# Gates behind the last SSD projection, transposes ahead of a q projection, and neighbouring blocks in one transfer: one layer of a streaming encoder trunk

## The chip, the cores and the metric

The kernel runs on one core of one Trainium2 chip. Its time is the device time of one launch, in microseconds (us), and a kernel's figure is the median of several launches. Engines are named as the profile names them: PE multiplies matrices, DVE is the vector engine, ACT the scalar engine (functions, copies with a scale), POOL and SP here only issue transfers (DMA). PEclk, or granted clock, is the share of full speed at which PE was allowed to run.

## The reference

One layer takes 576 tokens of width 1024 (512 of a prompt and 64 of a sample, with separate states and memories), and computes three branches from one normed input:

```python
h = _rmsnorm(x, norm_pre_w)
proj = h @ w_in
glu_v, glu_g, conv_gate, z, xbc, dt_raw, q, xa_gate, gates = jnp.split(proj, points, axis=-1)

u = glu_v * jax.nn.sigmoid(glu_g)
c, new_a = _causal_dwconv(u, st_a, conv_dw_w, conv_dw_b)      # width 31
c = jax.nn.silu(_layernorm(c, conv_ln_w, conv_ln_b)) * jax.nn.silu(conv_gate)
out_a = c @ conv_out_w
...
yg = yg * lax.rsqrt(jnp.mean(yg * yg, axis=-1, keepdims=True) + EPS)
y = yg.reshape(bsz, t, D_INNER) * ssd_norm_w.astype(f32)
out_b = y.astype(x.dtype) @ ssd_out_w
...
p = jax.nn.softmax(s, axis=-1)                                # 4 heads of 256, 256 memory tokens
o = jnp.einsum('bhtm,bmhd->bthd', p, mem_v.astype(f32)).reshape(bsz, t, XA_DIM).astype(x.dtype)
out_c = (o * jax.nn.silu(xa_gate)) @ xa_out_w

g = jax.nn.sigmoid(gates + gate_b).reshape(bsz, t, N_BRANCH, D_MODEL)
m = g[:, :, 0] * out_a + g[:, :, 1] * out_b + g[:, :, 2] * out_c
x_new = x + _rmsnorm(m @ w_out, norm_post_w)
```

Everything is float32. The states of both convolutions and of the scan, and keys and values of the memory, are outputs too.

## The kernel before

**Arithmetic.** Every float32 operand of a large product is split into a high part, rounded to the type fp32r, and a low part, the rest; a product is the sum of three matmuls (high by high, high by low, low by high). A projection takes 128 output channels for all tokens: 8 blocks of the inner dimension, 3 matmuls each, in two halves of 288 tokens, 48 matmuls (L214, `proj`) into one PSUM tile `mm`, of which there are two. So a projection waits until the tile of the one before the last has been read out. The right sides `hT` are the transposed normed input, high and low.

**Weights.** `wjob` puts a block of weights on the list `order`; `prep_to` works that list off, two blocks ahead of PE: SP fetches 512 KB into `raw` (three buffers), ACT rounds it into `whi` (L189), and the low part `wlo` comes either from a subtraction on DVE (L191) or from a negated copy on ACT (L193) with a DMA behind it that POOL issues and that adds `raw` to it (L194).

**Stages.** RMSNorm and transposes come first, then the four groups of the SSD branch with other projections between them, to about 510 us. The branch ends with four output projections `out_b(3, q)`. Two jobs stand behind these (L857 to L866): a projection each for `cg0` and `cg1`, the first blocks of the conv gate, of which a silu is made and stored in DRAM. Their silu is a tanh on ACT (L862) and a multiplication on DVE (L863) that reads the PSUM tile too:

```python
nc.scalar.activation(v2(t), va(pt), AF.Tanh, scale=0.5)
nc.vector.scalar_tensor_tensor(v2(t), v2(t), 1.0, va(pt), ALU.add, ALU.mult)
```

**Pairs** (516 to 726 us). Seventeen pairs of 128-column blocks of `w_in` are multiplied by a 2 by 2 block scheme with seven products, P1 to P7, of 12 matmuls each (L937, `product`), in place of eight. The products are summed in the PSUM tiles X, Y and Z, two of each. `slot` runs one product and the reading of its tile (on ACT or DVE, into tiles `ct`, `zs`, `ys`); `seq` lists the 119 slots, in which P2 of the next pair comes ahead of P7 of the present one. Ahead of the products, `pair_load` (L897) fetches the blocks into `raw` and `rawb` (four transfers of 256 KB a pair). `pair_pure` splits a block that enters a product as it is: P1, P2 and P4 have their high part `ph` from ACT (L907), and their low part `pl` from a negated copy on ACT (L908) and an adding DMA of POOL. `pair_sum` makes the sums of blocks that P5, P6, P7 and P3 need: four sums on DVE (L916), two splits on ACT (L919) and DVE (L920).

**Background.** The depthwise convolution is eight channel blocks with 31 taps and a first step each, one DVE instruction a tap (L791). `push_conv` puts its steps on a list, and `bgrun(n)` gives out n of them at the place where it stands; in the pairs that is `if i % 3: bgrun(1)`, in two of three slots.

**Attention** (740 to 880 us). For each head h: `att_kq` (two key projections, each followed by a q projection), `att_pt` for the head before (transposes of its softmax P on PE, L1212 and L1219, and the copies out of PSUM `pth` L1215, `ptl` L1216, `pts` L1221), `att_k` (transposes of keys, L1125 and L1177), `att_out` for the head before (products with the values, L1151 to L1153, L1235), and `att_scores`. A fifth turn ends the fourth head; there `fill` runs projections `cg2` to `cg4` in place of keys.

**Merge, LayerNorm, tail.** Eight merges (L1297, L1298) bring the attention branch into the accumulator `ob`, each with `bgrun(5)`. Eleven late projections follow, the rest of the conv gate `cg` and of the gate `g0` of the conv branch; a `cg` becomes a silu (tanh L474, multiplication L475/L476), a `g0` a tanh. Among them LayerNorm over the channels of the convolution: `ln_mean` sums all channels, and their squares, by matmuls with ones (L1309, L1310), `ln_rstd` takes the root on ACT (L1327) and the reciprocal on DVE (L1328). Then for each of eight channel blocks: multiply (L1359), tanh (L1362), three more DVE steps, and the split in high (L616) and low (L620) parts, on which the conv output projections `oa` work. `out_rows` ends the kernel.

**What sets the order.** The code is written in one sequence, and a scheduler with a simulated timeline then sets the order of the instructions on each engine; `bgrun` steps have a priority of their own. So instructions may stand on an engine some places before or behind where the code has them, and the order of each engine is shown where it matters.

Of the kernel before, what the change touches and what calls it, by code (L numbers as in the profile page):

```python
# [28 lines left out]
def hybrid_trunk_kernel(  # L29
# [829 lines left out]
    for j in range(2):
        pt = proj(f"cg{j}")  # L860
        t = sx.tile([128, 640], F32, tag="bc", name="bc", bufs=4)[:, 0:T]
        nc.scalar.activation(v2(t), va(pt), AF.Tanh, scale=0.5)  # L862
        nc.vector.scalar_tensor_tensor(v2(t), v2(t), 1.0, va(pt), ALU.add, ALU.mult)  # L863
# [24 lines left out]
    def pair_load(p):  # L888
        kind, i = pairs[p]
        cs = (C_GG + 128 * i, C_GV + 128 * i) if kind == "glu" else (base[kind] + 256 * i, base[kind] + 256 * i + 128)  # L890
        for kh in range(2):
# [4 lines left out]
            for n in range(2):  # L896
                nc.sync.dma_start(  # L897
                    out=raw[:, 512 * n:512 * n + 512].rearrange("p (k c) -> p k c", k=4),
                    in_=w_in[512 * kh:512 * kh + 512, cs[n]:cs[n] + 128].rearrange("(k p) c -> p k c", p=128),
                )  # L900
                pw[p][f"W{n + 1}{kh + 1}"] = raw[:, 512 * n:512 * n + 512]

    def pair_pure(p, w, pr):
        src = pw[p][w]
# [3 lines left out]
        nc.scalar.activation(lo, src, AF.Copy, scale=-1.0)  # L908
# [131 lines left out]
    for i, (p, pr) in enumerate(seq):  # L1040
# [469 lines left out]
```

## Time and profile before

| | us |
|---|---|
| three runs | 1125.15, 1127.86, 1120.45 |
| median | 1125.15 |
| the profiled execution | 1124.0 |
| its span in the trace | 1122.3 |
| mean granted clock of its core | 0.994 |
| ACT busy | 614.7 |
| POOL busy | 152.9 |

The profile is of a fourth execution. Its span goes from the first to the last recorded work of the core. A row of a group reads: line, engine, operation, output tile `<-` input tiles, count, then busy time. In brackets behind a row of the chain of waits stands how long the engine was idle ahead of it and what ended that. A row that lists the waits of PE has the total in us, how often, and the longest. Windows list for each engine its busy time and, as x, the instructions that began there, then the granted clock, the share of time in which the DMA engines were busy, and GB/s.

### The profile page before, as it was taken

To read this page: it belongs to the slowest core of one execution; us is meant where nothing else is said; L and a number is where in the kernel's file an instruction comes from. 1 tells how busy PE (TensorE), PEld (TensorE's weight loads), DVE (VectorE), ACT (ScalarE), POOL (GpSimd) and SP (SyncE) were. 2 spreads that over 40 slices of the span, in tenths; PEclk is the share of its full clock that TensorE was granted. 3 is DMA by queue.
4 is the path that set the end of the run, shared out by engine and by line. 5 is a ranking of instruction groups with operands and counts; after the bars stand their busy time and mean duration, and the time that the engine had idled before them with its cause. 6 is when DMAs were issued, how large, how long until landed. Compare 5 with 4: busy or idle time off the path is not lost. (4 is left out here: it accounts for less than half of the span.)

```text
span 1122.3 us, 20511 instructions
## 1 busy us (share of the span) xinstructions
PE 1091.3 (97%) x8081; PEld 1047.8 (93%) x8081; DVE 852.6 (76%) x1353; ACT 614.7 (55%) x1086; POOL 152.9 (14%) x247
## 2 busy tenths in 40 slices
PE   8999999999999999998999999999999999999997
PEld 8999999999999999998999999999999999999974
DVE  5778898578878984698898897669888789575533
ACT  5664675456436543745666656645655633675431
POOL 0100120012002100312323422100000111111000
PEclk9999999999999999998999999999999999999999
DMA  7354433442353235679797698666558698677812
GB/s 208 95 165 118 144 111 103 128 118 80 95 146 96 87 82 131 148 168 211 160 246 175 146 229 211 160 193 171 151 153 198 152 279 199 152 169 177 253 39 84
DMA packets 204086, 172.03 MB, mean 153 GB/s; under 512 B 15222, under 2 KB 176030, under 8 KB 203990
## 3 DMA queue, kind: packets, MB, share of 16 engines
q1 hardware_dynamic: 188006, 128.18, 39.5%
q0 software_dynamic: 14544, 39.59, 19.6%
q10 hardware_dynamic: 1440, 2.95, 0.7%
q8 instruction: 63, 1.03, 0.4%
q14 instruction: 33, 0.27, 0.1%
HBM read 116.49 MB, written 14.62 MB: 117 GB/s over the span
## 5 line engine op out<-in xcount | busy, mean ns | idle before, releaser
L214 PE MATMUL mm<-hT,whi 128*128 128x288 f32 (+2 forms) x2240 | 398.7, 298 | 2.9 <-DVE hi L476 1.3
L214 PEld LDWEIGHTS mm<-hT,whi 128*128 128x128 f32 x2240 | 334.5, 189 | 6.1 <-issue 1.5
L214 PE MATMUL mm<-hT,wlo 128*128 128x288 f32 (+2 forms) x1120 | 247.2, 298 | 0.2 <-DMA wlo<-raw 0.2
L189 ACT ACTIVATE whi<-raw 128x1024 fp32r<-128x1024 f32 x118 | 124.7, 1056 | 200.4 <-PE mm L214 157.6
L791 DVE SCALAR_TENSOR_TENSOR c<-u,dww,c 128x606 f32<-128x606 f32 x240 | 200.4, 844 | 2.5
L214 PEld LDWEIGHTS mm<-hT,wlo 128*128 128x128 f32 x1120 | 185.0, 189 | 1.3 <-issue 0.5
L191 DVE TENSOR_TENSOR wlo<-raw,whi 128x1024 fp32r<-128x1024 f32 x68 | 83.0, 1220 | 43.4 <-ACT whi L189 43.0
L214 PE MATMUL mm<-hi,whi 128*128 128x288 f32 x512 | 111.4, 299 | 0.3 <-DVE lo L1297 0.3
L214 PE MATMUL mm<-lo,whi 128*128 128x288 f32 x512 | 110.6, 296 | 0.0
L214 PE MATMUL mm<-hi,wlo 128*128 128x288 f32 x512 | 110.2, 296 | 0.0
L194 POOL DMA_DIRECT2D wlo<-raw x50 | 43.7, 873 | 396.5 <-ACT wlo L193 311.4
L214 PEld LDWEIGHTS mm<-hi,whi 128*128 128x128 f32 x512 | 82.4, 188 | 1.7 <-issue 1.1
L214 PEld LDWEIGHTS mm<-lo,whi 128*128 128x128 f32 x512 | 82.8, 188 | 0.0
L214 PEld LDWEIGHTS mm<-hi,wlo 128*128 128x128 f32 x512 | 82.7, 188 | 0.0
L193 ACT ACTIVATE wlo<-raw 128x1024 fp32r<-128x1024 f32 x50 | 52.4, 1048 | 16.1 <-PE ps L214 15.1
L466 DVE SCALAR_TENSOR_TENSOR acc<-xp,scw,acc 128x579 f32<-128x579 f32 x72 | 58.3, 813 | 3.1 <-ACT acc L462 1.9
L907 ACT ACTIVATE ph<-rawb 128x512 fp32r<-128x512 f32 x34 | 21.5, 632 | 56.5 <-PE X L937 29.9
L920 DVE TENSOR_TENSOR wlo<-sm,whi 128x1024 fp32r<-128x1024 f32 x34 | 41.4, 1219 | 7.3 <-ACT whi L919 7.3
L458 POOL COPY tails<-xp 128x3 f32<-128x3 f32 x24 | 18.9, 789 | 191.0 <-ACT xp L456 185.9
L919 ACT ACTIVATE whi<-sm 128x1024 fp32r<-128x1024 f32 x34 | 35.9, 1055 | 10.7 <-PE X L937 5.8
L909 POOL DMA_DIRECT2D pl<-rawb x34 | 29.6, 870 | 79.2 <-ACT pl L908 48.5
L937 PE MATMUL X<-hT,ph 128*128 128x288 f32 x136 | 28.7, 304 | 4.2 <-DVE bc L863 4.2
(373 smaller groups left out, 2257.1 us busy)
## 6 DMA issues: line engine op xcount, KB each, us to landing
raw<-in_w_in_dram SPq DMA_DIRECT2D x70, 512.0 KB
wlo<-raw POOLq DMA_DIRECT2D x50, 512.0 KB, 5.4
raw<-in_w_in_dram SPq DMA_DIRECT2D x34, 256.0 KB
rawb<-in_w_in_dram SPq DMA_DIRECT2D x34, 256.0 KB
pl<-rawb POOLq DMA_DIRECT2D x34, 256.0 KB, 4.3
R<-scr SPq DMA_DIRECT2D x16, 512.0 KB
raw<-in_ssd_out_w_dram SPq DMA_DIRECT2D x16, 512.0 KB
raw<-in_xa_kv_w_dram SPq DMA_DIRECT2D x16, 512.0 KB
```

Source lines behind the costliest of these rows:

```text
L189: a = nc.scalar.activation(hi[:, :n_], raw[:, :n_], AF.Copy)
L191: b = nc.vector.tensor_tensor(lo[:, :n_], raw[:, :n_], hi[:, :n_].bitcast(F32), ALU.subtract)
L193: nc.scalar.activation(lo[:, :n_], raw[:, :n_], AF.Copy, scale=-1.0)
L194: nc.gpsimd.dma_start(out=lo[:, :n_], in_=raw[:, :n_], accum_op=ALU.add)
L214: m = nc.tensor.matmul(o, lhsT=w, rhs=r[:, s:s + w_], start=(i == 0 and a == 0), stop=(i == n - 1 and a == 2),)
L466: nc.vector.scalar_tensor_tensor(acc, xp[:, r:r + 579], w4[:, r, jt:jt + 1], acc, ALU.mult, ALU.add)
L791: nc.vector.scalar_tensor_tensor(c, upad[j][:, r:r + NC], w31[:, r, j:j + 1], c, ALU.mult, ALU.add)
L907: nc.scalar.activation(hi, src, AF.Copy)
L909: nc.gpsimd.dma_start(out=lo, in_=src, accum_op=ALU.add)
L919: nc.scalar.activation(hi, sm, AF.Copy)
L920: nc.vector.tensor_tensor(lo, sm, hi.bitcast(F32), ALU.subtract)
L937: nc.tensor.matmul(o, lhsT=w[:, k], rhs=r[:, k], start=(start and k == 0 and a == 0), stop=(k == 3 and a == 2), skip_group_check=True,)
```

## The change

It has five parts.

1. Behind the last SSD output projection, `cg0` and `cg1` with their silu are replaced by `g0_0` and `g0_1`, which `gate_t` turns into a tanh on ACT and stores in DRAM. The conv gate keeps `cg0` to `cg2` for the fills, and the late list becomes `cg3` to `cg7`, then `g0_2` to `g0_7`: again eleven.
2. The transposes of P for the head before stand ahead of the second q projection (`mid` in `att_kq`), not behind it. In the fifth turn the fills stand around them, all three ahead of `att_out`.
3. A pair of neighbouring blocks (all but the glu pairs) is fetched in one transfer of 256 columns, 512 KB, for each half of the inner dimension. Blocks become views of three dimensions.
4. The low part of P2 is a subtraction on DVE; P1 and P4 keep the copy and the DMA.
5. Counts of background steps: `bgrun(3)` for 4 behind the SSD output projections, none where 6 stood behind each of the two gates, one in two slots instead of two in three in the first 60 slots of the pairs, 3 for 2 in half of the score steps, 6 for 5 in the merges. `ln_mean` and `ln_rstd` stand elsewhere among the late projections, and the two stored gates are loaded back behind `ln_mean`.

```diff
     for q in range(4):
         out_b(3, q)
-        bgrun(4)
+        bgrun(3)
     st.close()
     for j in range(2):
-        pt = proj(f"cg{j}")
-        t = sx.tile([128, 640], F32, tag="bc", name="bc", bufs=4)[:, 0:T]
-        nc.scalar.activation(v2(t), va(pt), AF.Tanh, scale=0.5)
-        nc.vector.scalar_tensor_tensor(v2(t), v2(t), 1.0, va(pt), ALU.add, ALU.mult)
-        nc.scalar.dma_start(out=spill["cg"][j], in_=t)
-        bgrun(6)
+        t = gate_t(f"g0_{j}", 0, j, sx, "bc", 4)
+        nc.scalar.dma_start(out=spill["g0"][j], in_=t)
...
+            else:
+                rv = raw.rearrange("p (k c) -> p k c", k=4)
                 nc.sync.dma_start(
-                    out=raw[:, 512 * n:512 * n + 512].rearrange("p (k c) -> p k c", k=4),
-                    in_=w_in[512 * kh:512 * kh + 512, cs[n]:cs[n] + 128].rearrange("(k p) c -> p k c", p=128),
+                    out=rv, in_=w_in[512 * kh:512 * kh + 512, cs[0]:cs[0] + 256].rearrange("(k p) c -> p k c", p=128)
                 )
-                pw[p][f"W{n + 1}{kh + 1}"] = raw[:, 512 * n:512 * n + 512]
+                for n in range(2):
+                    pw[p][f"W{n + 1}{kh + 1}"] = rv[:, :, 128 * n:128 * n + 128]
...
         nc.scalar.activation(hi, src, AF.Copy)
-        nc.scalar.activation(lo, src, AF.Copy, scale=-1.0)
-        nc.gpsimd.dma_start(out=lo, in_=src, accum_op=ALU.add)
+        if pr == "P2":
+            nc.vector.tensor_tensor(lo, src, hi.bitcast(F32), ALU.subtract)
+        else:
+            nc.scalar.activation(lo, src, AF.Copy, scale=-1.0)
+            nc.gpsimd.dma_start(out=lo, in_=src, accum_op=ALU.add)
...
-        if i % 3:
+        if i % (2 if i < 60 else 3):
             bgrun(1)
...
-    def att_kq(h):
+    def att_kq(h, mid):
...
             kfs.append(kv_proj(f"k{2 * h + i}", i, khi, klo))
+            if i == 1:
+                mid()
             src = va(q0[i] if h == 0 else proj(f"q{2 * h + i}"))
...
-            bgrun(2)
+            bgrun(3 if tp < 2 else 2)
...
         if h < 4:
-            khi, klo, ck, qhi, qlo, kfs = att_kq(h)
-        else:
-            fill(2)
-        if last is not None:
-            b_ = att_pt(h - 1, last[1])
+            khi, klo, ck, qhi, qlo, kfs = att_kq(h, pt_last)
+        else:
+            fill(0)
+            fill(1)
+            pt_last()
...
         pt = proj(oname, act=act)
-        bgrun(5)
+        bgrun(6)
...
     for e in late[:2]:
         late_job(*e)
         bgrun(5)
     bgrun(10000)
     late_job(*late[2])
-    late_job(*late[3])
     ln_mean()
-    for e in late[4:6]:
+    for j in range(2):
+        g0t.append(hlA.tile([128, T], F32, tag="lo", name="lo", bufs=8))
+        nc.sync.dma_start(out=g0t[j], in_=spill["g0"][j])
+    for e in late[3:6]:
         late_job(*e)
+    ln_rstd()
     late_job(*late[6])
-    ln_rstd()
```

How it stands on the engines at the places that the prediction speaks of (line, operation, output `<-` inputs, shape; xN for N in a row):

DVE where the SSD branch ends and the pairs begin, before. L916 are sums for the first pairs, L920 their low parts, L791 conv taps, L863 the two silus:

```order
L916 TENSOR_TENSOR sm<-sm,rawb 128x512
L920 TENSOR_TENSOR wlo<-sm,whi 128x1024
L863 SCALAR_TENSOR_TENSOR bc<-bc,mm 128x576
L791 SCALAR_TENSOR_TENSOR c<-u,dww,c 128x606 x2
L916 TENSOR_TENSOR sm<-raw,rawb 128x512
L920 TENSOR_TENSOR wlo<-sm,whi 128x1024
L791 SCALAR_TENSOR_TENSOR c<-u,dww,c 128x606 x2
L916 TENSOR_TENSOR sm<-sm,raw 128x512
L863 SCALAR_TENSOR_TENSOR bc<-bc,mm 128x576
```

The same place after (L923 are the sums, L927 their low parts, L913 the new low part of P2):

```order
L791 SCALAR_TENSOR_TENSOR c<-u,dww,c 128x606 x3
L913 TENSOR_TENSOR pl<-rawb,ph 128x512
L923 TENSOR_TENSOR sm<-raw,rawb 128x512
L923 TENSOR_TENSOR sm<-raw 128x512
L923 TENSOR_TENSOR sm<-sm,raw 128x512
L913 TENSOR_TENSOR pl<-rawb,ph 128x512
L923 TENSOR_TENSOR sm<-sm,rawb 128x512
L927 TENSOR_TENSOR wlo<-sm,whi 128x1024
L923 TENSOR_TENSOR sm<-raw,rawb 128x512
L927 TENSOR_TENSOR wlo<-sm,whi 128x1024
L923 TENSOR_TENSOR sm<-sm,raw 128x512
```

The silus are gone, and with them the taps between the sums; the low parts of P2 of the first two pairs stand between the sums.

ACT at that place, before (L919 rounds sums, L862 is the tanh of the two silus, L864 the store):

```order
L919 ACTIVATE whi<-sm 128x1024
L862 ACTIVATE bc<-mm 128x576
L919 ACTIVATE whi<-sm 128x1024
L864 DMA spill_cg<-bc 128x576
L862 ACTIVATE bc<-mm 128x576
L919 ACTIVATE whi<-sm 128x1024
L864 DMA spill_cg<-bc 128x576
```

And after (L926 rounds sums, L749 is the tanh of the gate, L861 the store):

```order
L926 ACTIVATE whi<-sm 128x1024
L749 ACTIVATE bc<-mm,half 128x576
L926 ACTIVATE whi<-sm 128x1024
L861 DMA spill_g_108<-bc 128x576
L926 ACTIVATE whi<-sm 128x1024
L749 ACTIVATE bc<-mm,half 128x576
L861 DMA spill_g_108<-bc 128x576
```

The order stays; a tanh of `g0` stands where a tanh of `cg` stood, with a rounding of sums ahead of each.

PE in attention where the first head's P is transposed, before. L214 with `hT` is the end of the second q projection of the next head, L1212 and L1219 are the transposes, L1125 and L1177 those of the keys:

```order
L214 MATMUL mm<-hT_92,whi 128x288 x2
L214 MATMUL mm<-hT_93,whi 128x288 x2
L214 MATMUL mm<-hT_92,wlo 128x288 x2
L1212 MATMUL ps<-ident,P 128x128 x8
L1219 MATMUL ps<-ident,P 128x64 x2
L1125 MATMUL ps<-ident,kf 128x128 x4
L1177 MATMUL ps<-ident,ck 128x128 x4
L1151 MATMUL ps<-pth,vvh 128x512
L1152 MATMUL ps<-ptl,vvh 128x512
```

And after (L214 with `memT` is the second key projection, L1221 and L1228 are the transposes of P):

```order
L214 MATMUL ps<-memT_8487,wlo 128x256
L214 MATMUL ps<-memT_8487,whi 128x256
L214 MATMUL ps<-memT_8488,whi 128x256
L214 MATMUL ps<-memT_8487,wlo 128x256
L1221 MATMUL ps<-ident,P 128x128 x8
L1228 MATMUL ps<-ident,P 128x64 x2
L214 MATMUL mm<-hT_92,whi 128x288 x2
L214 MATMUL mm<-hT_93,whi 128x288 x2
L214 MATMUL mm<-hT_92,wlo 128x288 x2
```

The q projection has moved from ahead of the transposes to behind them, between them and the products that need their copies.

ACT behind LayerNorm's second sum, before. L1327 is the root, L189 and L193 round weights, L475 the tanh of `cg7`, L749 that of a `g0` gate, L1362 the tanh of a normed channel block, L616 its high part:

```order
L1327 ACT_TABLE_LOAD
L1327 ACTIVATE mean<-ps,eps_78 128x288 x2
L189 ACTIVATE whi<-raw 128x1024
L475 ACT_TABLE_LOAD
L475 ACTIVATE hi<-mm 128x576
L193 ACTIVATE wlo<-raw 128x1024
L1362 ACTIVATE th<-u,half 128x576 x2
L189 ACTIVATE whi<-raw 128x1024
L749 ACTIVATE lo<-mm,half 128x576
L193 ACTIVATE wlo<-raw 128x1024
L1362 ACTIVATE th<-u,half 128x576 x2
L616 ACTIVATE hi<-hi 128x576 x2
```

And after (L1340 is the root, L1374 the tanh of a block):

```order
L1340 ACT_TABLE_LOAD
L1340 ACTIVATE mean<-ps,eps_78 128x288 x2
L189 ACTIVATE whi<-raw 128x1024
L749 ACT_TABLE_LOAD
L749 ACTIVATE lo<-mm,half 128x576
L193 ACTIVATE wlo<-raw 128x1024
L1374 ACTIVATE th<-u,half 128x576 x2
L189 ACTIVATE whi<-raw 128x1024
L749 ACTIVATE lo<-mm,half 128x576
L193 ACTIVATE wlo<-raw 128x1024
L1374 ACTIVATE th<-u,half 128x576 x2
```

On PE the second sum (L1310, after L1323) comes, before, in the projection of `cg7`: 32 of its matmuls and `g0_5`, `g0_6`, `g0_7` stand between the sum and the first `oa`. After, it comes in `g0_6`: 32 matmuls of that and `g0_7` stand there. So of the gates on ACT three `g0` and one `cg` follow the root before, and two `g0` after.

More of the change, by code (lines that the diff above doesn't have):

```diff
@@ L90, in hybrid_trunk_kernel @@
     msc = dram.tile([8, 128, T], F32, name="msc")
-    spill = {k: dram.tile([8, 128, T], F32, name=f"spill_{k}") for k in ("xg", "g2", "cg")}
+    spill = {k: dram.tile([8, 128, T], F32, name=f"spill_{k}") for k in ("xg", "g2", "g0")}
     scr = dram.tile([5, 32, 128], F32, name="scr")
@@ L144, in hybrid_trunk_kernel @@
     for j in range(2):
-        wjob(f"cg{j}", w_in, C_CG + 128 * j)
+        wjob(f"g0_{j}", w_in, C_G + 128 * j)
     hold = len(order)
@@ L156, in hybrid_trunk_kernel @@
             wjob(f"v{h}_{n}", xa_kv_w, 1024 + 256 * h, r0=512 * n, kk=4, cols=256)
-    for j in range(2, 5):
+    for j in range(3):
         wjob(f"cg{j}", w_in, C_CG + 128 * j)
@@ L160, in hybrid_trunk_kernel @@
         wjob(f"oc{j}", xa_out_w, 128 * j)
-    late = [("cg", 5), ("cg", 6)] + [("g0_", j) for j in range(5)] + [("cg", 7)] + [("g0_", j) for j in range(5, 8)]
+    late = [("cg", j) for j in range(3, 8)] + [("g0_", j) for j in range(2, 8)]
     for k, j in late:
@@ L745, in gate_t @@
     def gate_t(name, br, j, pool, tag, bufs):
-        t = pool.tile([128, T], F32, tag=tag, name=tag, bufs=bufs)
+        t = pool.tile([128, 640 if tag == "bc" else T], F32, tag=tag, name=tag, bufs=bufs)[:, 0:T]
         pt = proj(name)
@@ L921, in pair_sum @@
         for q, pr in enumerate(prs):
-            pw[p][pr] = hi[:, 512 * q:512 * q + 512], lo[:, 512 * q:512 * q + 512]
+            pw[p][pr] = [w[:, 512 * q:512 * q + 512].rearrange("p (k c) -> p k c", k=4) for w in (hi, lo)]
     pb = [{} for _ in pairs]
@@ L931, in product @@
     def product(p, pr, tag, start):
-        wh, wl = (w.rearrange("p (k c) -> p k c", k=4) for w in pw[p][pr])
+        wh, wl = pw[p][pr]
         rh, rl = rhs[pr]
@@ L1245, in fill, with pt_last @@
         bgrun(4)
+    b_ = []
+    def pt_last():
+        if last is not None:
+            b_[:] = att_pt(h - 1, last[1])
     for h in range(5):
         if h < 4:
-            khi, klo, ck, qhi, qlo, kfs = att_kq(h)
+            khi, klo, ck, qhi, qlo, kfs = att_kq(h, pt_last)
         else:
-            fill(2)
-        if last is not None:
-            b_ = att_pt(h - 1, last[1])
+            fill(0)
+            fill(1)
+            pt_last()
         if h < 4:
@@ L1256, in hybrid_trunk_kernel @@
         else:
-            fill(3)
+            fill(2)
         if last is not None:
@@ L1261, in hybrid_trunk_kernel @@
             last = att_scores(h, khi, klo, qhi, qlo, ckh, ckl)
-        else:
-            fill(4)
     for b in range(2):
@@ L1331, in hybrid_trunk_kernel @@
         merge(j, 2, None, f"oc{j}", ocact)
-    sgs = {2 + i: t for i, t in enumerate(sgl)}
+    sgs = dict(enumerate(sgl))
     chl, g0t = [], []
@@ L1339, in late_job @@
             g0t.append(gate_t(f"g0_{j}", 0, j, hlA, "lo", 8))
-    for j in range(2):
-        sgs[j] = hlA.tile([128, T], F32, tag="hi", name="hi", bufs=8)
-        nc.sync.dma_start(out=sgs[j], in_=spill["cg"][j])
     for e in late[:2]:
```

14 lines of the change are left out of this document (10 added, 4 removed).

## The prediction, made before the changed kernel ran

> **What bounds the kernel now.** I read the page first, then windows along the span, the waits of PE (the matmul engine), the tail in order of time, and the groups by line.
>
> ```profile
> span 1122.3 us, 20511 instructions
> PE 1091.3 (97%) x8081; PEld 1047.8 (93%) x8081; DVE 852.6 (76%) x1353; ACT 614.7 (55%) x1086; POOL 152.9 (14%) x247
> ```
>
> PE is the bound: it stands for 1122.3 - 1091.3 = 31.0 us. No matmul is removed, so the change can gain only from those 31 us and from matmuls that run at a lowered clock. The waits of PE name who is late.
>
> ```profile
> PE Z L937 <- DMA pl<-rawb: 5.0, 4, 1.6
> PE X L937 <- DVE bc L863: 4.2, 1, 4.2
> PE ps L1177 <- ACT pts L1221: 1.7, 2, 0.8
> ...
> PE mm L214 <- DVE hi L476: 1.3, 1, 1.3
> ...
> PE ps L1151 <- ACT pts L1221: 1.1, 1, 1.1
> ...
> PE Z L937 <- DVE bc L863: 0.6, 1, 0.6
> PE ps L1152 <- DVE ptl L1216: 0.6, 1, 0.6
> ...
> PE ps L1151 <- ACT kk L1127: 0.5, 1, 0.5
> ```
>
> The columns are total us, times and longest. Five groups are touched: the gates behind the last SSD projection (L863, 4.8), the pair product P2 that waits for its low half (5.0), attention (L1177, L1151, L1152: 1.7 + 1.1 + 0.6 + 0.5 = 3.9), and one wait behind LayerNorm (1.3). What a stall costs beyond its idle time shows in windows of 4 us of PE alone (busy and matmuls, granted clock, DMA):
>
> ```profile
> 516.00:520.00 4.00, 1.84 (x12) 1.00 1.04 246
> 520.00:524.00 4.00, 1.54 (x6) 0.61 0.30 99
> 524.00:528.00 4.00, 4.00 (x20) 0.53 0.89 205
> 528.00:532.00 4.00, 4.00 (x32) 1.00 0.93 199
> ...
> 608.00:612.00 4.00, 2.52 (x11) 0.71 0.77 190
> 612.00:616.00 4.00, 4.00 (x28) 0.87 0.42 104
> ...
> 692.00:696.00 4.00, 2.52 (x19) 1.00 1.11 265
> ```
>
> A full window holds 32 or 33 matmuls. After the L863 wait the clock falls to 0.61 and 0.53, and the first three windows are 20.5 + 26.5 + 12.5 = 59.5 short. One matmul takes 76.80 / 576 = 0.133 us by the chain of waits, a projection of 48 thus 6.4 us:
>
> ```profile
> 887.93 76.80 PE mm L214 x576
> ```
>
> So the L863 wait costs 59.5 x 0.133 = 7.9 us, not 4.8; the stall at 608 costs (21.5 + 4.5) x 0.133 = 3.5 us, of which 1.5 is idle time and 2.0 the clock. The equally long stall at 692 left the clock at 1.00. DVE, the vector engine, is the second bound:
>
> ```profile
> core 0: us, PE busy (x) PEld busy (x) DVE busy (x) ACT busy (x) POOL busy (x), PEclk, DMA share, GB/s
> ...
> 620.00:640.00 20.00, 19.88 (x150) 19.64 (x149) 17.37 (x29) 13.42 (x25) 8.21 (x9) 1.00 0.69 153
> 640.00:660.00 20.00, 20.00 (x152) 19.94 (x151) 18.59 (x28) 12.32 (x23) 6.00 (x6) 1.00 0.84 187
> 660.00:680.00 20.00, 18.03 (x134) 17.56 (x133) 15.41 (x23) 13.04 (x25) 4.33 (x5) 1.00 0.89 215
> 680.00:700.00 20.00, 18.28 (x136) 17.81 (x135) 18.71 (x28) 11.87 (x22) 4.32 (x5) 1.00 0.88 237
> ```
>
> **The change, part by part.** *Gates behind the SSD projection.* A sigmoid gate needs only a tanh on ACT to free its PSUM tile; the silu it replaces also needed L863, which stood on DVE behind taps and sums. All 7.9 us could go. But in ACT's new order a whi conversion stands ahead of the second tanh, and it waits for two DVE sums of the next pair; by DVE's new order and 0.68 a sum I put that tanh about 1.2 us later than X wants its bank. I take 6.5; ends 4.5 (X waits 3 us) and 7.9.
>
> *P2's low half on DVE, larger transfers.* Seventeen copies on ACT and as many accumulating DMAs go, seventeen DVE subtractions come:
>
> ```profile
> L916 DVE TENSOR_TENSOR sm<-raw,rawb x17: 680/683/693, 509.8 to 695.9; 128x512 f32<-128x512 f32 x17
> ```
>
> ```profile
> L908 ACT ACTIVATE pl<-rawb x34: 612/616/637, 509.2 to 703.8; 128x512 fp32r<-128x512 f32 x34
> ...
> DMA to landing us min/median/max: 3.2/4.2/7.1
> ```
>
> The chain behind the high half was 0.62 + 4.2 us and becomes 0.68 (a subtraction of the same size; the strided source is not in this trace, between 0.68 and twice that, and the nearest row is the plain one). A gain in wait is sure, a gain in time is not, since it loads DVE by 0.68 a pair. A pair is seven products of 12 matmuls, 84 x 0.133 = 11.2 us. In the first half of the pairs every second slot instead of two in three gives a conv tap, 3.5 instead of 4.7 a pair, which makes up for it; there the 3.5 us at 608 go. In the second half nothing is relieved: DVE's 17.37 + 18.59 + 15.41 + 18.71 = 70.1 us between 620 and 700 become 70.1 + 7 x 0.68 = 74.9, while PE's some 565 matmuls there need 75.3. The remaining three waits (5.0 - 1.5 = 3.5) I let shrink by 0.8 only, the rest comes back as waits for DVE. Together 4.3; ends 7.0 and, with DVE as the bound, -2. The merged transfers cost and gain nothing: before a P2 conversion ACT waits for PE to free its tile, not for the load; if that cover were gone, P2 would wait for 512 KB in place of 256.
>
> *Transposes ahead of the q projection.* The copies behind them (pts, pth, ptl) now have 6.4 us of PE work over them in three of four heads. Of 3.9 I take 3.6; ends 1.5 (the reordered DVE queue delivers late) and 3.9.
>
> *Conv taps later.* Four slots lose one each, two gates six each, the pair slots ten: 26 steps move behind the pairs. Eight go to attention, eight to the merges, the rest is drained before LayerNorm.
>
> ```profile
> 939.26 0.85 DVE L791 SCALAR_TENSOR_TENSOR c<-u,dww,c 128x606 f32<-128x606 f32 x1
> 940.03 0.75 DVE L1297 SCALAR_TENSOR_TENSOR bc<-bc,mm 128x576 f32<-128x576 f32 x1
> ```
>
> ```profile
> 740.00:960.00 220.00, 215.92 (x1642) 211.10 (x1641) 184.77 (x273) 113.41 (x202) 19.02 (x22) 1.00 0.74 185
> ```
>
> A tap holds DVE 940.03 - 939.26 = 0.77 us, so 20 us move into a stretch where DVE stands for 220 - 184.8 = 35 us. A merge with six taps needs 6 x 0.77 + 2 x 0.67 = 6.0 of its 6.4 us. I cost them at nothing; their cover is that idle time and the later place of LayerNorm. With no fill between the last head and the first merge, PE meets the split of oc about 0.6 us early: -0.6; ends -0.3 and -2.
>
> *LayerNorm two projections later.* This is the term against the change. In the new PE order the sum of squares stands behind 9 of the 11 late projections, where it stood behind 7; 32 matmuls and one projection are left before the conv output projections need the normed channels, instead of 32 and three.
>
> ```profile
> 986.67 0.42 PE L1310 MATMUL ps<-sl,onesr 128*128 128x288 f32 x2
> ```
>
> ```profile
> 989.08 3.75 DVE L1328 RECIPROCAL mean<-mean 128x576 f32<-128x576 f32 x1 [5.77 <-ACT mean L1327]
> 992.87 5.44 DVE L1359 TENSOR_TENSOR u<-u,mean 128x576 f32<-128x576 f32 x8
> ...
> 1003.53 0.74 DVE L620 SCALAR_TENSOR_TENSOR lo<-hi 128x576 fp32r<-128x576 f32 x1
> ...
> 1019.53 0.76 DVE L620 SCALAR_TENSOR_TENSOR lo<-hi 128x576 fp32r<-128x576 f32 x1 [0.75 <-ACT hi L616]
> 1024.38 1.42 DVE L1297 SCALAR_TENSOR_TENSOR lo<-lo,mm 128x576 f32<-128x576 f32 x2 [4.09 <-PE mm L214]
> ```
>
> Call R the end of the second sum, 987.1. The first channel block is split at 1004.3 = R + 17.2, the last at 1020.3 = R + 33.2, and the first two output projections end at 1024.3 = R + 37.2. Before, PE had 32 + 3 x 48 = 176 matmuls = 23.5 us of cover, so it ran into nothing. Now it has 80 = 10.7 us: PE stands from R + 10.7 for about 5 us and is then paced by DVE, one block about each 2 to 3 us against 1.6 us of matmuls, up to the last block at R + 32 (one silu less on DVE). The two projections end near R + 34.2. R itself comes 96 matmuls = 12.8 us later. The term is 12.8 + 34.2 - 37.2 = -9.8; the 1.3 us wait for L476 is in the 37.2. Ends: -8.4 (last block at R + 31.8 with 1.1 us of matmuls behind it) and -13 (the low clock adds the 3.1 us that it added at 520).
>
> *Sum.* 6.5 + 4.3 + 3.6 - 0.6 - 9.8 = 4.0 us. The profiled execution took 1124.0 us (span 1122.3, 1.7 around it), so 1120.0; that execution lies 1.15 below the median 1125.15 of the three runs, which range over 7.4.
>
> By the Trainium skill, "TensorE: Matmul & The Clock Gate", Part 1, the clock halves after about 3.4 us without work, in windows that run free, and recovers after as long a busy stretch. By that rule 1.5 us of idling at 608 would cost no clock, the stall there would be worth 1.5 instead of 3.5, and the sum would be 2.0 us, 1122.0. The trace has both: 0.71 at 608, 1.00 at 692. I keep the row. The same rule speaks against the new gap behind LayerNorm.
>
> **Rivals.** *Faster: every stall goes.* 7.9 + 7.0 + 3.9 - 0.3 - 8.4 = 10.1, 1113.9 us. For it: each wait has one named cause that is taken away. Against it: DVE at 74.9 of 75.3.
>
> *DVE becomes the bound in the pairs.* In 640 to 660 PE was full and DVE still idled 1.4 us, waiting for others. If those gaps stay, 18.6 + 1.2 + 1.4 = 21.2 us are needed for 20, 6% over 8.5 pairs of 11.2 us, 5.7 us lost instead of 0.8 won: 1126.5. It decides from about 0.2 us more per pair.
>
> *Slower: PE waits for LayerNorm's first sum.* If DVE's 35 us of idle time are waits that recur, the 20 us of moved taps push the last tap back. The new place of the sum gives 1.2 projections = 7.7 us, less the 3.6 us by which attention gets shorter, and some 2.4 were spare: 6.5. The rest, 13.5, is a stall of PE, with 3 of clock: 1136.5. It decides once DVE uses less than 13.5 of its 35 us. Against it: six taps fit into a merge.
>
> *The tail is covered after all,* if the blocks come in time: 1110. The order speaks against it, since 10.7 is less than 17.2.
>
> **How the numbers follow.** Forecast 0.47, with its own range 1115 to 1125; faster 0.20; DVE in the pairs 0.17; LayerNorm's sum 0.11; tail covered 0.05. The predicted time is 1120.0. Leaving out the outer parts of the fast cases and most of the slowest gives 1110 to 1131. About 1% is what a measurement of this kernel can tell from no change, so from 1125.15 faster means under 1113.9 and slower over 1136.4. Half of the fast case and the covered tail, with a little of the forecast, make 0.18; half of the slowest and a little of the DVE case 0.08; within 1% stays 0.74.
>
> **What would show it.** Right: no wait of PE for DVE at the first X, clock 1.00 there; no Z wait for a DMA; no wait for pts in attention; and a wait of 4 to 6 us of the first conv output projection for an ACT or DVE split, then a low clock. Wrong: that wait absent or over 8 us; waits of Z, X or Y for DVE above 4 us together in the pairs; a wait at LayerNorm's first sum.

## The result, and the profile after

The changed kernel is slower: 1133.39 us, median of six runs (1130.76 to 1135.67), against 1124.99 for six runs of the kernel before. The ratio is 1.0076, with a 95% interval of 1.0054 to 1.0099: 6 to 11 us lost where 4 were forecast as a gain, and above the stated range. The page of the changed kernel (profiled execution 1130.76 us):

```profile
span 1129.0 us, 20428 instructions
...
PE 1094.6 (97%) x8081; PEld 1050.1 (93%) x8081; DVE 863.8 (77%) x1370; ACT 607.9 (54%) x1069; POOL 142.3 (13%) x230
```

PE is still the bound and its matmuls are the same 8081, but it idles 34.4 us instead of 31.0, and is busy 3.3 us longer with the same matmuls, at a mean granted clock of 0.992 instead of 0.994. The waits of PE in the changed kernel (total us, times, longest):

```profile
PE mm L214 <- ACT hi L616: 4.6, 1, 4.6
PE mm L214 <- DMA wlo<-raw: 3.2, 1, 3.2
PE X L944 <- ACT bc L749: 2.4, 1, 2.4
PE Y L944 <- DVE wlo L927: 2.3, 1, 2.3
PE X L944 <- ACT u L1005: 2.2, 3, 1.2
PE Z L944 <- DVE pl L913: 2.0, 4, 0.8
PE mm L214 <- DVE lo L620: 2.0, 2, 1.3
...
PE Y L944 <- ACT whi L926: 1.5, 2, 0.8
```

Every wait that the change was to remove is gone or small: no wait for L863, for an adding transfer of P2, for pts. In their place stand the one that was forecast (L616 and L620, behind LayerNorm), one for weights in the merges (wlo, 3.2), one for the tanh of the new gate (2.4) and 8.0 us spread over X, Y and Z in the pairs. Of these waits in the pairs 4.8 us are for DVE (2.3, 2.0 and one of 0.5 for `ct`), more than the 4 us that the prediction named as a sign of being wrong; e7 shows what that sign was worth. Where the time went, by the starts of the last or first instruction of a group in both traces, of one execution each:

| stage | its end before | its end after | gain | forecast |
|---|---|---|---|---|
| to the last product of the pairs | 725.4 | 723.4 | 2.0 | 6.5 + 4.3 |
| attention, to the first matmul of the merges | 887.7 | 881.9 | 3.8 | 3.6 |
| merges, to the last one on DVE | 940.0 | 937.2 | -3.0 | -0.6 |
| late projections, LayerNorm, tail (span) | 1122.3 | 1129.0 | -9.5 | -9.8 |
| sum | | | -6.7 | 4.0 |

So the tail, the largest loss, came as forecast, and attention too. What failed is the pairs, by 8.8 us, and a smaller part in the merges. The windows of PE at the start of the pairs, then behind LayerNorm:

```profile
516.00:520.00 4.00, 1.59 (x12) 1.00 1.02 238
520.00:524.00 4.00, 4.00 (x22) 0.67 0.74 187
524.00:528.00 4.00, 4.00 (x30) 0.90 0.60 118
528.00:532.00 4.00, 4.00 (x33) 1.00 0.97 187
```

```profile
1008.00:1012.00 4.00, 0.64 (x5) 1.00 0.68 128
1012.00:1016.00 4.00, 2.10 (x7) 0.61 0.94 241
1016.00:1020.00 4.00, 4.00 (x20) 0.53 0.48 97
```

From 516 to 532 the changed kernel has 97 matmuls and the kernel before 70; with the window ahead of these, 32 and 29, that is 30 x 0.133 = 4.0 us won. From there to the end of the pairs it wins nothing more and loses 2.0. The first X now waits for the tanh on ACT:

```profile
518.12 1.06 ACT L926 ACTIVATE whi<-sm 128x1024 fp32r<-128x1024 f32 x1 [2.24 <-DVE sm L923]
...
519.08 0.72 ACT L749 ACTIVATE bc<-mm,half 128x576 f32<-128x576 f32 x1
```

The rounding of sums ahead of it waited 2.24 us for DVE. That is the order that the prediction read; it put the tanh 1.2 us late, and PE stood 2.4 us for it.

Behind LayerNorm, the chain of waits in order of time, and PE's own row:

```profile
999.97 3.76 DVE mean L1341
...
1003.76 5.44 DVE u L1371 x8
...
1024.49 0.68 DVE lo L620
...
1025.21 5.93 PE mm L214 x40
```

```profile
1013.19 1.33 PE L214 MATMUL mm<-hi,whi 128*128 128x288 f32 x4 [4.56 <-ACT hi L616]
```

and DVE's last two low parts:

```profile
1027.92 1.43 DVE L620 SCALAR_TENSOR_TENSOR lo<-hi 128x576 fp32r<-128x576 f32 x2
```

Call R' the end of the second sum here, 998.0. PE stopped 10.6 us behind it, stood 4.6 us, and went on at the pace of DVE's blocks. The last block for which PE waited was split at 1025.2 = R' + 27.2, the last of all at 1029.35 = R' + 31.4, where the forecast had R + 32. In the three windows PE did 32 of some 97 matmuls: idle time and a clock of 0.53 to 0.61 together.

### The profile page after: what moved, and what is told of

It reads as the page before. It is cut to its first block, busy times and chain, and to the rows that moved or that the text cites. A ratio compares the mean times of both kernels' runs of the same rounds, so it can differ in the third digit from the quotient of the medians.

```text
span 1129.0 us, 20428 instructions
## 1 busy us (share of the span) xinstructions
PE 1094.6 (97%) x8081; PEld 1050.1 (93%) x8081; DVE 863.8 (77%) x1370; ACT 607.9 (54%) x1069; POOL 142.3 (13%) x230
## 4 chain that ended last, share of the span: by engine, by line
PE 80%; DVE 7%; DMA 5%; issue 5%; ACT 3%; SPq 0%; POOL 0%; DVEq 0%; ACTq 0%; POOLq 0%
PE mm L214 50%; PE X L944 7%; PE ps L214 4%; PE Y L944 4%; PE ps L1159 2%; PE ps L1158 2%; PE ps L1160 2%; PE ps L573 2%; PE Z L944 2%; PE ps L599 2%; DMA wlo<-raw 1%; PE ps L577 1%; DMA msc<-ob 1%; DMA rawb<-in_w_in_dram 1%; DMA ob<-in_x_prompt_dram 1%
## 5 line engine op out<-in xcount | busy, mean ns | idle before, releaser
L214 PE MATMUL mm<-hT,whi 128*128 128x288 f32 (+2 forms) x2240 | 398.4, 298 | 1.5 <-DVE sz L476 0.6
L214 PEld LDWEIGHTS mm<-hT,whi 128*128 128x128 f32 x2240 | 334.4, 189 | 5.0 <-issue 1.5
L214 PE MATMUL mm<-hT,wlo 128*128 128x288 f32 (+2 forms) x1120 | 246.8, 298 | 0.0
L189 ACT ACTIVATE whi<-raw 128x1024 fp32r<-128x1024 f32 x118 | 124.7, 1057 | 210.5 <-PE mm L214 162.4
L791 DVE SCALAR_TENSOR_TENSOR c<-u,dww,c 128x606 f32<-128x606 f32 x240 | 199.7, 846 | 2.6
L214 PEld LDWEIGHTS mm<-hT,wlo 128*128 128x128 f32 x1120 | 184.9, 189 | 0.7 <-issue 0.5
L214 PE MATMUL mm<-hi,whi 128*128 128x288 f32 x512 | 112.1, 301 | 4.9 <-ACT hi L616 4.6
L214 PE MATMUL mm<-hi,wlo 128*128 128x288 f32 x512 | 111.2, 298 | 3.2 <-DMA wlo<-raw 3.2
L214 PE MATMUL mm<-lo,whi 128*128 128x288 f32 x512 | 112.0, 299 | 2.1 <-DVE lo L620 2.0
L214 PEld LDWEIGHTS mm<-hi,whi 128*128 128x128 f32 x512 | 83.1, 191 | 6.5 <-ACT hi L616 4.8
L214 PEld LDWEIGHTS mm<-hi,wlo 128*128 128x128 f32 x512 | 83.6, 190 | 3.5 <-DMA wlo<-raw 3.5
L214 PEld LDWEIGHTS mm<-lo,whi 128*128 128x128 f32 x512 | 83.6, 190 | 3.2 <-DVE lo L620 2.8
L193 ACT ACTIVATE wlo<-raw 128x1024 fp32r<-128x1024 f32 x50 | 52.4, 1049 | 18.4 <-PE ps L214 17.4
L927 DVE TENSOR_TENSOR wlo<-sm,whi 128x1024 fp32r<-128x1024 f32 x34 | 41.5, 1221 | 11.3 <-ACT whi L926 11.3
L926 ACT ACTIVATE whi<-sm 128x1024 fp32r<-128x1024 f32 x34 | 35.9, 1055 | 10.6 <-PE X L944 7.4
L916 POOL DMA_DIRECT2D pl<-raw x17 | 20.2, 1187 | 86.5 <-ACT pl L915 61.7
```

Of the source, the lines that this page charges most:

```text
L189: a = nc.scalar.activation(hi[:, :n_], raw[:, :n_], AF.Copy)
L193: nc.scalar.activation(lo[:, :n_], raw[:, :n_], AF.Copy, scale=-1.0)
L214: m = nc.tensor.matmul(o, lhsT=w, rhs=r[:, s:s + w_], start=(i == 0 and a == 0), stop=(i == n - 1 and a == 2),)
L791: nc.vector.scalar_tensor_tensor(c, upad[j][:, r:r + NC], w31[:, r, j:j + 1], c, ALU.mult, ALU.add)
L926: nc.scalar.activation(hi, sm, AF.Copy)
L927: nc.vector.tensor_tensor(lo, sm, hi.bitcast(F32), ALU.subtract)
```

## The experiments

All times are medians; each ratio is to runs of the kernel before on the same chip. 1% is 11.2 us.

| run | what it is | us | ratio, 95% interval |
|---|---|---|---|
| - | the changed kernel | 1133.4 | 1.0076 (1.0054 to 1.0099) |
| e1 | memory scaling later | 1128.9 | 1.0051 (1.0024 to 1.0078) |
| e2 | counts of background steps as before | 1125.4 | 1.0024 (1.0004 to 1.0043) |
| e3 | low half of P2 by transfer | 1179.9 | 1.0499 (1.0461 to 1.0537) |
| e4 | two transfers a block | 1126.7 | 1.0025 (1.0004 to 1.0046) |
| e5 | two transfers, new layout | 1131.3 | 1.0062 (1.0036 to 1.0088) |
| e6 | memory load and scaling later | 1130.9 | 1.0059 (1.0038 to 1.0080) |
| e7 | e2 and e4 together | 1112.5 | 0.9901 (0.9872 to 0.9931) |
| e12 | e7, new layout | 1123.2 | 0.9996 (0.9978 to 1.0014) |
| e8 | before, P2 on DVE alone | 1120.8 | 0.9976 (0.9955 to 0.9997) |
| e9 | before, transposes alone | 1118.8 | 0.9943 (0.9921 to 0.9965) |
| e10 | before, gates alone | 1116.9 | 0.9917 (0.9890 to 0.9945) |
| e11 | e7, loads of `ob` spread | 1110.4 | 0.9854 (0.9814 to 0.9895) |

**e1, the scaling of the memory tokens later.** In the changed kernel PE loses 5.6 us between 572 and 588, and there DVE stands 4.9 us at the scaling of `ob` (L1045), which waits for its load.

```diff
-            nc.vector.tensor_scalar(m_t, m_t, ssm[:, t, 2:3], None, ALU.mult)
+            nc.vector.tensor_scalar(m_t, m_t, sml[:, t:t + 1], None, ALU.mult)
...
+                nc.vector.scalar_tensor_tensor(
+                    sml[:, t:t + 1], pb[9]["z"][:, 0:1], 0.0, ssm[:, t, 2:3], ALU.mult, ALU.add
+                )
```

> The changed kernel, but the scaling of the memory tokens on DVE (in the changed kernel it waited 4.9 us at the head of DVE's queue, at 572 to 577 us) is tied to a later pair, so that it stands about 70 rows further back on DVE; its two transfers stay where they are. Theory A (that wait is what the pairs lose between 572 and 588): PE's loss of some 5.5 us there goes, 1128 us, 5 us less than the changed kernel's 1133.4. Rival B (the low half of P2 loads DVE to its limit): DVE catches up nothing, the stalls move on within the pairs, within 1.5 us of 1133.4. Rival C (blocks of 512 KB land too late for ACT): the stalls of ACT for rawb remain, 8 of them, and at most 2 us are gained.

In time it lies between the two, with an interval that overlaps the changed kernel's. The trace is against theory A: the loss moves (PE is short of full windows from 568 to 592, and waits 3.0 us for L1005 once), and the last product starts at 723.5, as in the changed kernel. DVE's wait was not by itself the cause.

**e2, the taps.** Five edits, such as

```diff
-        bgrun(3)
+        bgrun(4)
...
-        if i % (2 if i < 60 else 3):
+        if i % 3:
```

> The changed kernel with all counts of background steps of the kernel before (part 5 of the change undone, and the steps behind the two gates put back). LayerNorm's second sum has 171 matmuls of cover behind it again instead of 80. Theory D (the moved taps cost LayerNorm 9.5 us): PE's waits for L616 and L620 (4.6 + 2.0 us) vanish and the tail from the last merge is 9 to 10 us shorter; if ten more taps in the pairs cost nothing, 1124 us. Rival B (DVE is at its limit in the pairs): each tap that comes back into the pairs costs 0.8 us there, up to 8 us, and the whole is 1130 to 1132.

The waits for L616 and L620 are gone, and from the last merge to the end the span takes 1119.5 - 938.5 = 181.0 us instead of 191.8, 10.8 less. Only the counts went back, not the places of `ln_mean` and `ln_rstd`, so it was the late taps that had put the sum late. The pairs end 3.6 us later (727.0), with ten more taps in them; with two transfers a block the same taps cost 1.3 there (716.9 in e4, 718.2 in e7). Theory D holds, and B in a part: 8.0 us between the medians, 5.8 by the ratios, hang on where the taps are.

**e3 and e4, the low half of P2 and the transfers.** In e3

```diff
-        if pr == "P2":
-            nc.vector.tensor_tensor(lo, src, hi.bitcast(F32), ALU.subtract)
-        else:
-            nc.scalar.activation(lo, src, AF.Copy, scale=-1.0)
-            nc.gpsimd.dma_start(out=lo, in_=src, accum_op=ALU.add)
+        nc.scalar.activation(lo, src, AF.Copy, scale=-1.0)
+        nc.gpsimd.dma_start(out=lo, in_=src, accum_op=ALU.add)
```

> The changed kernel with the low half of P2 by a copy on ACT and an adding transfer again (part 4 undone). Rival B (DVE load): 17 x 0.69 = 11.7 us of DVE work leave the pairs; the pairs end some 5 us earlier, 1128. Theory A: the wait of DVE for the memory tokens stays, and waits of Z for the transfer of 1 to 1.6 us come back, 3.5 to 5 us in all: 1135 to 1138.

and in e4

```diff
-            if kind == "glu":
+            if True:
                 rv = raw.rearrange("p (n k c) -> p n k c", n=2, k=4)
```

> The changed kernel with two transfers of 256 KB in place of each one of 512 KB (part 3 undone). Rival C: ACT's eight waits for rawb (32 us idle in all) shrink as the first half lands about 2 us earlier, and PE gains 3 to 5 us in the pairs: 1129. Theories A and B: within 1.5 us of 1133.4.

e3 was expected by neither theory: 46 us slower than the changed kernel, nearly all of it one kind of wait:

```profile
PE Z L941 <- DMA pl<-rawb: 42.9, 13, 10.7
```

The same transfers cost 5.0 us in four waits in the kernel before. So in the changed kernel an adding transfer is a different thing. e4 points to the new loads: with two transfers a block the pairs end at 716.9 instead of 723.4. POOL's issue of the adding transfers and ACT's high halves between 515 and 726, of the changed kernel (busy, mean ns of one, idle time before and its causes):

```profile
L916 POOL DMA_DIRECT2D pl<-rawb x17 | 20.0, 1175 | 68.3 <-PE X L944 13.5 <-ACT ph L911 12.3 <-DMA spill_g<-bc 6.9
...
L911 ACT ACTIVATE ph<-rawb 128x512 fp32r<-128x512 f32 x31 | 19.6, 632 | 50.1 <-DMA rawb<-in_w_in_dram 21.1 <-PE X L944 17.2 <-PE Z L944 11.1
```

and of e4:

```profile
L916 POOL DMA_DIRECT2D pl<-rawb x17 | 14.8, 870 | 50.7 <-ACT pl L915 18.3 <-PE X L944 18.0 <-DVE sm L923 14.5
...
L911 ACT ACTIVATE ph<-rawb 128x512 fp32r<-128x512 f32 x31 | 19.6, 631 | 39.8 <-PE X L944 23.5 <-PE Z L944 10.0 <-DMA rawb<-in_w_in_dram 5.8
```

POOL's queue from 515 to 715 (packets, MB, share of the DMA engines) and the landing of its transfers in us, of the changed kernel and then of e4:

```profile
q0 software_dynamic: 13968, 8.65, 34.5%
...
pl<-rawb POOLq DMA_DIRECT2D x17, 256.0 KB, 4.4
```

```profile
q0 software_dynamic: 4837, 9.06, 26.8%
...
pl<-rawb POOLq DMA_DIRECT2D x17, 256.0 KB, 3.3
```

The large transfer leaves the 512 numbers of a product in four pieces of 128. The adding transfers of P1 and P4 read them so: three times the packets for no more bytes, 1.18 us of POOL's queue for 0.87, and 1.1 us more to land. SP refills `rawb` only when P4's transfer has read it (it waits 82.3 us for such transfers in this stretch, and 67.8 in e4), so the weights come late, and ACT waits 21.1 us for them instead of 5.8. The engines themselves read the pieces as fast as the rows: ACT's high halves take 632 ns against 631, DVE's sums 685 to 689 against 683 to 688. Two things changed at once, though, size and layout.

**e5 and e12, the layout alone.** Two transfers of 256 KB, into the places of the large one; e12 has the counts of e2 as well:

```diff
-                nc.sync.dma_start(
-                    out=rv, in_=w_in[512 * kh:512 * kh + 512, cs[0]:cs[0] + 256].rearrange("(k p) c -> p k c", p=128)
-                )
                 for n in range(2):
+                    nc.sync.dma_start(
+                        out=rv[:, :, 128 * n:128 * n + 128],
+                        in_=w_in[512 * kh:512 * kh + 512, cs[n]:cs[n] + 128].rearrange("(k p) c -> p k c", p=128),
+                    )
```

> The changed kernel with two transfers of 256 KB a block again, but into the same places as the large one: the 512 numbers that a product reads lie in four pieces of 128 in each partition, as in the changed kernel, while in the run with two transfers they lay in one piece. Theory C1 (what costs is the size of the transfer: P2 waits for 512 KB): as fast as the run with two transfers, 1126.7 us, and ACT's waits for rawb shrink to about 6 us. Theory C2 (what costs is the layout: the adding transfers of P1 and P4 read pieces of 512 bytes instead of rows of 2 KB, have 14,000 packets instead of 4,800 in the pairs, land a us later and hold rawb longer): as slow as the changed kernel, 1133.4 us, with POOL's issues still at 1.2 us instead of 0.87.

> The faster kernel (two transfers, counts as before, ratio to the kernel before 0.9901), with the layout of the changed kernel: two transfers of 256 KB into the places of the large one. Its counterpart with the large transfer had 1.0024. Theory C2 (the layout costs, through the adding transfers of P1 and P4): near the counterpart, 1.000 to 1.002, 1123 to 1127 us, with the waits of PE in the pairs back and 14,000 packets of the adding transfers. Theory C1 (the size costs): near the faster kernel, 0.990 to 0.993, 1112 to 1116. In between, in parts: both.

POOL's rows of e5 are those of the changed kernel:

```profile
q0 software_dynamic: 14000, 8.78, 34.3%
...
pl<-rawb POOLq DMA_DIRECT2D x17, 256.0 KB, 4.4
```

Layout takes the ratio from 1.0025 (e4) to 1.0062 (e5), and from 0.9901 (e7) to 0.9996 (e12): 0.0037 and 0.0095. The intervals of e4 and e5 overlap, those of e7 and e12 don't. ACT's waits for `rawb` go the same way: 5.8 us in e4 and 15.9 in e5, 0.5 in e7 and 18.6 in e12. The larger transfer on top takes the ratio to 1.0076 and 1.0024: 0.0014 and 0.0028, within the intervals. So C2 holds for about three quarters of the loss; whether size costs anything by itself stays unclear. The large transfer into the old layout wasn't tried, nor the new layout with the low halves of P1 and P4 on DVE, which would show whether the loss goes through the adding transfers alone.

**e6, the load of the memory tokens later too.** As e1, with the scaling tied to pair 11, and a small DVE instruction that reads `ob` and a tile of pair 7 holds back `mem_load`.

```diff
+                nc.vector.scalar_tensor_tensor(
+                    sm0[:, t:t + 1], pb[7]["z"][:, 0:1], 0.0, obf[:, D * t:D * t + 1], ALU.mult, ALU.add
+                )
             mem_load()
```

> The changed kernel with both the load of the memory tokens and their scaling tied to later pairs (7 and 11), so that SP issues the load where no store of ob is under way. In the run with the scaling alone moved, the pairs still lost some 7 us between 568 and 592, where SP stood up to 5.4 us behind a load that waits for a store of ob. Theory A2 (it is SP's wait that delays the weights of the next pair): the loss between 568 and 592 goes, the pairs end 4 to 6 us earlier, 1128. Theory C2 alone (layout): the loss stays or moves by one pair, 1132 to 1134.

The time, 1130.9, lies between what the two theories gave, but the pairs end at 723.2, as in the changed kernel. A2 falls as A did: with the layout of the changed kernel the loss finds another place.

**e7, both undone together** (the edits of e2 and e4).

> The changed kernel with two transfers of 256 KB a block and with the counts of background steps of the kernel before; left of the change are the gates, the low half of P2 on DVE and the transposes. If the two undone parts are independent, 1133.4 - 6.7 - 8.0 = 1118.7 us, faster than the kernel before. If DVE becomes the bound in the pairs once the ten taps are back (rival B), 1122 to 1125, with waits of PE for DVE above 4 us in the pairs.

Below the 1118.7 us of two independent gains, and faster than the kernel before by 8 to 14 us. Its page, and the sum row of the windows from 620 to 700, of the changed kernel and then of e7:

```profile
span 1112.3 us, 20463 instructions
...
PE 1087.7 (98%) x8081; PEld 1044.3 (94%) x8081; DVE 862.3 (78%) x1370; ACT 607.2 (55%) x1069; POOL 140.0 (13%) x230
```

```profile
sum 80.00, PE 76.17 PEld 74.69 DVE 72.16 ACT 50.47 POOL 19.80; mean PE 19.04 PEld 18.67 DVE 18.04 ACT 12.62 POOL 4.95
```

```profile
sum 80.00, PE 78.96 PEld 78.26 DVE 76.36 ACT 52.24 POOL 18.81; mean PE 19.74 PEld 19.56 DVE 19.09 ACT 13.06 POOL 4.70
```

DVE does 76.4 us of work in 80 and PE still 79.0. Rival B, that DVE bounds the pairs, falls: with weights in time DVE runs at 95%, and PE waits for it 0.5 us in all the pairs, against 4.8 in the changed kernel.

**e8, e9, e10, the good parts one by one in the kernel before.** e8 is the diff of e3 backwards. e9:

```diff
             kfs.append(kv_proj(f"k{2 * h + i}", i, khi, klo))
+            if i == 1:
+                mid()
...
-        if last is not None:
-            b_ = att_pt(h - 1, last[1])
```

e10, with the fills, the late list and the places of `ln_mean` and `ln_rstd` that belong to it:

```diff
-        nc.scalar.activation(v2(t), va(pt), AF.Tanh, scale=0.5)
-        nc.vector.scalar_tensor_tensor(v2(t), v2(t), 1.0, va(pt), ALU.add, ALU.mult)
-        nc.scalar.dma_start(out=spill["cg"][j], in_=t)
+        t = gate_t(f"g0_{j}", 0, j, sx, "bc", 4)
+        nc.scalar.dma_start(out=spill["g0"][j], in_=t)
         bgrun(6)
```

> The kernel before with one edit alone: the low half of P2 by a subtraction on DVE. By the prediction the waits for the adding transfer (5.0 us, and 2 of clock) go and about 4.3 us are gained, with 2.7 to 7 for the work that DVE has too much, so 1119 to 1122 where the kernel before has 1124. Rival B: the taps at two in three slots and the subtraction together exceed DVE's time, nothing is gained or up to 4 us lost, 1124 to 1128.

> The kernel before with one edit alone: the transposes of P ahead of the second q projection. By the prediction PE's waits for pts, ptl and kk in attention (3.9 us) go but for some 0.3: 3.6 us, with 1.5 to 3.9, so 1120.4 where the kernel before has 1124.0. Rival (copies and products then meet other work on ACT and DVE): the waits return at other lines of attention, nothing gained, 1123 to 1125.

> The kernel before with the tanh gates in place of the silus alone, with the exchange of the fills and of the late list that goes with it; transfers, low half of P2, transposes and counts are those of the kernel before. By the prediction 6.5 us (4.5 to 7.9), 1117.5 where the kernel before has 1124.0. By the trace of the changed kernel, whose windows from 512 to 532 hold 30 matmuls more than those of the kernel before: 4.0 us, 1120.0. If the wait only moves from the silu to the tanh behind the sums' rounding: 1122 to 1124.

P2 gives 2.7 us (0.3 to 5.1), the transposes 6.4 (3.9 to 8.9), the gates 9.3 (6.2 to 12.4). These ratios hold all that an edit moves. By the end of the pairs e10's trace is 7.8 us ahead, and with attention, where the fills now stand otherwise, 6.0; of the 6.7 us that e9's trace gains, 4.6 lie in attention and 2.2 in the pairs, where the edit has no line. In e10 PE has no wait for a gate, and the windows behind the last SSD projection are all but full:

```profile
516.00:520.00 4.00, 4.00 (x33) 1.00 1.05 254
520.00:524.00 4.00, 4.00 (x33) 1.00 1.08 240
524.00:528.00 4.00, 3.87 (x29) 1.00 1.00 255
528.00:532.00 4.00, 4.00 (x31) 1.00 0.77 146
```

In the changed kernel the two low halves of P2 stand among the sums on DVE, and the rounding ahead of the tanh waits for DVE. In e3, where they come by transfer, PE waits 0.5 us for the tanh instead of 2.4, and the five windows from 512 to 532 hold 153 matmuls instead of 129. But e2, e7, e11 and e12 have the low halves on DVE too, with the counts as before, and hold 145 to 154. So the gate fell to 4.0 us where the low halves on DVE and the new counts came together; how the counts do it wasn't followed.

The three add up to 18.4 us and e7, which has all three, won 11.1. By the traces the difference lies in the pairs: 7.8 and 5.4 us for the gates and P2 alone, 7.2 together. That they share DVE's time there would explain it; no run shows it.

**e11, the wait in the merges.** In the changed kernel the eight loads of `ob` and the adding transfer of a block of weights, SP's row and POOL's:

```profile
891.31 3.68 SPq L1296 DMA_DIRECT2D ob<-msc  x8
...
894.97 0.87 POOL L194 DMA_DIRECT2D wlo<-raw  x1 [13.78 <-ACT wlo L193]
```

By the chain of waits that transfer took 10.45 us, behind 2.3 MB of loads.

```diff
-    for j in range(8):
+    for j in range(3):
         nc.sync.dma_start(out=ob[:, j], in_=msc[j])
...
+        if br == 2 and j < 5:
+            nc.vector.tensor_scalar(ob2[:, j + 3, 0:1], ob2[:, j, 0:1], 0.0, None, ALU.mult)
+            nc.sync.dma_start(out=ob2[:, j + 3], in_=msc[j + 3])
```

> The faster kernel (two transfers, counts as before) with five of the eight loads of the stored accumulator, 288 KB each, let go one by one behind the merges instead of all at once ahead of them; a DVE instruction of one number ties each to a merge. In the run of the faster kernel the low half of a block of the attention output weights stood behind these loads and landed 8.9 us after its issue, and PE waited 1.7 us (3.2 in the changed kernel). Theory E (the burst of loads causes it): that wait goes, the landing falls to 5 to 6 us, 1110 to 1111 where the faster kernel had 1112.5. Rival: the block is late by ACT's or POOL's order, the wait stays, 1112 to 1114.

The transfer lands 5.75 us after its issue instead of 8.94 in e7, PE has no wait for wlo left anywhere, and the kernel has the lowest time of all, 12 to 21 us under the kernel before. Theory E holds. That it beats e7 rests on the trace (the wait of 1.7 us is gone); the intervals of the two ratios overlap.

## Why the prediction was wrong, step by step

- **The step that failed: "The merged transfers cost and gain nothing: before a P2 conversion ACT waits for PE to free its tile, not for the load."** They cost 5.7 us (1.0076 to 1.0025, e4), and 13.8 where the taps are as before (1.0024 to 0.9901, e2 and e7). Of the 8.8 us by which the pairs fell short in the trace, e4 gives back 6.5. The step looked at one reader of the block, ACT's copy for P2. The others were not costed: the adding transfers of P1 and P4, whose source changed from one piece to four. Their rows were in the profile (0.87 us of POOL, 4.2 us to land), and the diff shows the new view. e5 and e12 show that this layout makes about three quarters of the loss. The cover that it named, PE's freeing of the tile, gave way to waits for `rawb` after the change (21.1 us on ACT), and the price of that, which the prediction set down in words as a wait for 512 KB, never entered the range.
- **P2's low half on DVE:** 4.3 forecast, 2.7 measured alone; right in direction and within its ends. The strided source, priced at 0.68 to twice that, took 0.685 us. The rival that DVE becomes the bound fell (e7).
- **Gates:** 6.5 forecast, 7.8 alone in the pairs, 4.0 in the changed kernel. The mechanism and the place of the lateness were right; how late ACT's tanh comes was put at half of what it was.
- **Transposes:** 3.6 forecast, 3.8 in the trace. Alone 6.4, with an interval (3.9 to 8.9) just above both; the trace of that run has 4.6 in attention.
- **Taps, at nothing:** short in the stretch itself by 2.3 to 2.7 us, which attention and merges together are shorter with the counts as before (e2 against the changed kernel, e7 against e4). Above all the taps set when LayerNorm's sum comes in the order of PE, so they are the same term as the next.
- **LayerNorm:** -9.8 forecast, -9.5 in the trace, and 10.8 won back by e2. The largest term of the sum, worked out from the order and the chain, was right in its mechanism: a stop at 10.6 us for 10.7, a wait of 4.6 for 5, the last block at 31.4 for 32. That it is right to 0.3 us has some luck in it: measured from the last merge the sum came 13.7 us later, not 12.8, and the tail behind it was 4.1 us shorter, not 3.0.
- **Merges:** -0.6 forecast, -3.0 measured. The eight loads now go out 3.7 us ahead of an adding transfer that PE needs; the prediction did not look at SP's queue there. In e11, with these loads spread, the merges are 1.9 us shorter than in e7.
- **The slowest rival, 1136.5,** lies near the measured time, but not by its mechanism: PE has no wait at LayerNorm's first sum.

Without that step the time would have been inside 1110 to 1131, but not at its middle: e4, which has all but the large transfers, lies 2.8 us above the kernel before, where the sum had 4.0 below. By its trace the merges hold 3.5 us of the rest and the pairs 2.3. The prediction speaks of five groups of waits and lists four; no term hangs on it.

## What to carry to other kernels

When a transfer's layout changes, list every reader of the tile, the transfers first, and compare their packets: fetching in fewer, larger transfers can turn another queue's rows into pieces. Background work that is pushed back is paid for where its result is needed, so cost it there, not where it runs. A part that is good alone can be hidden by another: three edits that each gain and two that each lose gave a kernel that loses.

## What the runs showed of the hardware

Adding transfers of 256 KB between places in SBUF, on POOL's queue, took 1.18 us of issue instead of 0.87 and 4.4 us to land instead of 3.3 when the source lay in pieces of 512 bytes instead of 2 KB. POOL's queue kept the DMA engines busy 34.5% of the stretch for 8.65 MB, where it took 26.8% for 9.06 MB. The Trainium skill, "DMA: Bandwidth & Descriptors", section "Why small descriptors are slow (HBM only)", says that transfers from SBUF to SBUF don't suffer from small descriptors; here, for the adding kind, they did.

The prediction left open why 1.5 us of standing at 608 cost clock and as much at 692 did not. In the traces the clock changes only in windows of 3.41 us, which lie on a fixed grid. PE alone in such windows of the kernel before (busy and matmuls, granted clock, DMA):

```profile
606.23:609.65 3.42, 1.75 (x12) 1.00 0.74 123
609.65:613.06 3.41, 3.25 (x13) 0.50 1.05 272
691.57:694.98 3.41, 2.95 (x23) 1.00 1.11 257
694.98:698.39 3.41, 2.27 (x17) 1.00 0.77 241
698.39:701.80 3.41, 3.41 (x28) 1.00 0.44 76
```

At 608 two waits, 0.35 and 1.48 us, fell almost wholly into one window, in which PE was idle for 49%; the wait of 1.6 us at 694.5 was split over two. Between 30 and 1085 us, the 14 traces have 28 windows at full clock in which PE was idle for 54% or more, and a window at 0.50 followed each of them; it followed 2 of 19 windows between 39% and 53%, and none below. So a wait of some 2 us costs clock or not by where it falls on the grid: the first X of the changed kernel left 55% of a window idle and cost clock, that of e7 46% and didn't. By the rule that the prediction took from the Trainium skill, "TensorE: Matmul & The Clock Gate", Part 1, a whole window of about 3.4 us without work halves the clock. The traces agree with it on the length of the window; a little over half a window of idle time was enough.
